# Gathered experts in a two-stream diffusion trunk: the weighted sum of the second halves moved from VectorE rows to TensorE column quarters

## The chip, the cores and the metric

One core of a Trainium2 chip runs the whole step in one launch. The metric is device time in microseconds (us). Several executions of the kernel before were timed; one more was recorded by the hardware profiler, and every row shown here is from that one.

## The reference, cut to what matters

Two layers serve a context stream (128 tokens) and a latent stream (512 tokens). Each layer has a token mixer (gated linear attention, short convolution, windowed attention, merged through three gated branches) and then a feed-forward step with 16384 tiny experts (PEER). Each token picks 16 experts in each of 8 heads, 128 in all; an expert is one row of `u_tab` and one row of `v_tab`, 1024 float32 each:

```python
def block(args):
    xb, ib, gb = args                      # tokens, expert numbers, gates
    act = gelu(einsum('td,thkd->thk', xb, u_tab[ib]))
    return einsum('thk,thkd->td', gb * act, v_tab[ib])
```

All data are float32, and the tables differ from layer to layer.

## The kernel before

The program is a Python generator under a tile scheduler: instructions are issued in the order of the text as far as their tiles are free, and each engine then runs its own queue in order. Long side jobs are generators of their own. `tick()` (called after each group of matmuls in the main work) moves a side job forward by its rate, a number of steps per tick.

Of the five blocks of 128 tokens (one of the context, four of the latents) two take the *gather* way in each layer: the context block and the first latent block. That makes four gathers. The other three latent blocks take the *dense* way (`peer_dense`, L1032 and on): for every pair of expert rows, TensorE forms the hidden values (`u_hidden`, 24 matmuls into a PSUM tile `pb`), multiplies them with a gate map `G`, splits them in two (`daH`, `daL`) and adds the second halves up in six PSUM accumulators (`down`, 18 matmuls per expert). Hidden values of the first 108 experts (layer 0) or 64 (layer 1) are formed ahead and come back from DRAM (`da<-sdr`) in the last part of that loop.

A gather (`peer_gather`, L880) has 128 tokens on the 128 partitions. For each of the 128 ranks j, `fetch` (L908) issues an indirect DMA on GpSimd's queue that brings row `eidx[:, j]` of a table, one row per token, into a buffer `grow` of 128 x 1024 (512 KB). A row of `u` is used on VectorE by `u_row` (L914): multiply with `h`, add up into column j of `w`; after 16 ranks ScalarE applies the Gelu. A row of `v` is used by `v_row` (L920): `acc = g * w[:, j] + acc`, again one VectorE instruction. The order is 16 rows of `u`, then rows of `u` and `v` of neighbouring heads in turn by sixteens; `fetch` runs `LAG` = 1 step ahead of the use (L1250), so a gather has 257 steps. Buffers: five `grow` (L1329, L1373), or, in the dense loop, the eight `wraw` buffers that the weights of the dense way use too (L1390).

Where the four gathers run:

- context, layer 0: beside the latents' mixer (`mixer_lat`, rates 0.9 in the linear attention, 5.5 in the attention, 2.464 in the branches), first fetch at 595 us, last use at 1480 us;
- first latent block, layer 0: beside the gate maps (`gate_map`, 48 ticks at a rate of 2.0), then beside the dense loop with a rate that makes it end some ten ticks before the loop (L1391), from 2282 to 3315 us;
- context, layer 1: beside the latents' mixer (rates 0.84, 6.0, 2.08), from 3392 to 4361 us;
- first latent block, layer 1: as in layer 0 (48 ticks and 30 more of `routing_pairs`, rate 1.056; then the dense loop), from 4596 to 5820 us.

PSUM has four kinds of tiles with two buffers each: `pa`, `po`, `pb`, `pt`. In the mixer `pt` takes transposes (those of the attention's probabilities above all); in the dense loop `pa`, `po` and `pt` are the accumulators, and only `pb` is free for hidden values.

Matmuls of the latents run on pairs of rounded halves (`mm3`, L192, three matmuls in place of one). Matmuls on plain float32 operands stand in the trace as two instructions (passes) each. One line of the kernel before, L401, multiplies 16 partitions at a time, once from partition 0 and once from partition 32.

Of the kernel before, what the change touches and what calls it, by code (L numbers as in the profile page):

```python
# [9 lines left out]
F32 = mybir.dt.float32  # L10
F32R = mybir.dt.float32r
BF16 = mybir.dt.bfloat16
I32 = mybir.dt.int32
U32 = mybir.dt.uint32
U8 = mybir.dt.uint8
AF = mybir.ActivationFunctionType
# [27 lines left out]
def kernel(ctx: ExitStack, tc: tile.TileContext, A: dict, O: list):  # L44
# [760 lines left out]
    def routing_pairs(t, vals, idxs, rp, qp, out):  # L805

        vf = vals[t].rearrange("p (h q) k -> p h q k", q=2)
        xf = qp.tile([128, 8, 2, 16], F32, name="xf", bufs=1)  # L810
        V.tensor_copy(xf.rearrange("p h q k -> p (h q k)"), idxs[t].rearrange("p h k -> p (h k)"))
        top = qp.tile([128, 8, 16], F32, name="top", bufs=1)
        pos = qp.tile([128, 8, 16], U32, name="pos", bufs=1)
        for h in range(8):
            cand = qp.tile([128, 136], F32, name="cand", bufs=1)
            V.tensor_add(cand[:, :128].rearrange("p (a b) -> p a b", b=16),
                         vf[:, h, 0, :8, None].to_broadcast([128, 8, 16]),
                         vf[:, h, 1, None, :].to_broadcast([128, 8, 16]))
            V.tensor_scalar(cand[:, 128:], vf[:, h, 0, 8:], vf[:, h, 1, 0:1], None, op0=OP.add)
            top16(top[:, h, :], pos[:, h, :], cand)  # L820
            if h % 2:
                yield
        pf = qp.tile([128, 8, 16], F32, name="pf", bufs=1)
        V.tensor_copy(pf, pos)
        ab = qp.tile([128, 2, 8, 16], U32, name="ab", bufs=1)
        V.tensor_scalar(ab[:, 0], pos, 4, None, op0=OP.logical_shift_right)
        V.tensor_scalar(ab[:, 1], pos, 15, None, op0=OP.bitwise_and)
        abf = qp.tile([128, 2, 8, 16], F32, name="abf", bufs=1)
        V.tensor_copy(abf, ab)

        V.tensor_scalar(pf, pf, -128.0, 0.0, op0=OP.add, op1=OP.max)
        V.tensor_add(abf[:, 0], abf[:, 0], pf)
        V.tensor_sub(abf[:, 1], abf[:, 1], pf)
        sel = rp.tile([128, 2, 8, 16], F32, name="sel%d" % t)
        yield
        for q in range(2):
            for h in range(8):
                oh = qp.tile([128, 16, 16], F32, name="oh", bufs=2)
                V.tensor_tensor(oh, abf[:, q, h, :, None].to_broadcast([128, 16, 16]),
                                iota16[:, None, :].to_broadcast([128, 16, 16]), op=OP.is_equal)  # L840
                nc.gpsimd.tensor_mul(oh, oh, xf[:, h, q, None, :].to_broadcast([128, 16, 16]))  # L841
                V.reduce_sum(sel[:, q, h, :], oh, axis=mybir.AxisListType.X)
                if h % 4 == 3:
                    yield
        flat3 = lambda v: v.rearrange("p h k -> p (h k)")
        eidx = None
        if t == 0:
            eidx = rp.tile([128, 8, 16], I32, name="eidx")
            V.scalar_tensor_tensor(eidx, sel[:, 0], 128.0, sel[:, 1], op0=OP.mult, op1=OP.add)
            eidx = flat3(eidx)  # L850
        gate = rp.tile([128, 8, 16], F32, name="gate%d" % t)
        V.tensor_sub(gate, top, top[:, :, 0:1].to_broadcast([128, 8, 16]))
        act(gate, gate, AF.Exp)
        gs = qp.tile([128, 8], F32, name="gs", bufs=1)
        V.reduce_sum(gs, gate, axis=mybir.AxisListType.X)
        V.reciprocal(gs, gs)
        V.tensor_mul(gate, gate, gs[:, :, None].to_broadcast([128, 8, 16]))
        out[t] = (eidx, flat3(gate), flat3(sel[:, 0]), flat3(sel[:, 1]))
        yield
# [20 lines left out]
    def peer_gather(s, l, t, eidx, gate, gp, out=None, after=None):  # L880
        h = gp.tile([128, D], F32, name="gh", bufs=1)
        def row():
            return gcfg["p"].tile([128, D], F32, tag=gcfg["tag"], name="grow", bufs=gcfg["n"])

        def mrow(j):
            t_ = row()
            m = modrow[l][s.idx, j * D:(j + 1) * D]
            nc.sync.dma_start(t_, bass.AP(tensor=m.tensor, offset=m.offset, ap=[[0, 128], [1, D]]))
            return t_

        sc, sh = mrow(4), mrow(3)
        x = s.x[t]
        if not s.ctx:
            x = row()
            nc.sync.dma_start(x, xdr[s.name][:, t, :])
        i = V.scalar_tensor_tensor(h, sc, 1.0, x, op0=OP.add, op1=OP.mult)
        if after:
            behind(i, after)
        V.tensor_add(h, h, sh)
        acc = gp.tile([128, D], F32, name="gacc", bufs=1)  # L900
        junk = gp.tile([128, D], BF16, name="gjunk", bufs=1)
        w = gp.tile([128, 128], F32, name="gw", bufs=1)

        def pin(i):
            if PIN[gcfg["m"]]:
                tc.keep_in_program_order(i)

        def fetch(tab, j):  # L908
            g = row()
            nc.gpsimd.indirect_dma_start(out=g, out_offset=None, in_=A[tab + str(l)],  # L910
                                         in_offset=bass.IndirectOffsetOnAxis(ap=eidx[:, j:j + 1], axis=0))
            return g

        def u_row(j, g):  # L914
            pin(V.scalar_tensor_tensor(junk, g, 1.0, h, op0=OP.mult, op1=OP.mult, accum_out=w[:, j:j + 1]))  # L915
            if j % 16 == 15:
                ws = w[:, j - 15:j + 1]
                act(ws, ws, AF.Gelu)

        def v_row(j, g):  # L920
            if j % 16 == 0:
                ws = w[:, j:j + 16]
                V.tensor_mul(ws, ws, gate[:, j:j + 16])
            if j == 0:
                pin(V.tensor_scalar(acc, g, w[:, j:j + 1], None, op0=OP.mult))
            else:
                pin(V.scalar_tensor_tensor(acc, g, w[:, j:j + 1], acc, op0=OP.mult, op1=OP.add))  # L927


        rows = []  # L930
        for hd in range(9):
            r = range(hd * 16, hd * 16 + 16)
            rows += [(u_row, "peer_u", j) for j in r if hd < 8] + [(v_row, "peer_v", j - 16) for j in r if hd]
        todo = []
        for i in range(len(rows) + LAG):
            if i < len(rows):
                todo.append(fetch(*rows[i][1:]))
            if i >= LAG:
                use, _, j = rows[i - LAG]
                use(j, todo.pop(0))  # L940
            yield
        if s.ctx:
            peer_add(s, t, [acc], mrow(5), acc)
            normalize(s, [t])
        else:
            out.append(acc)
# [300 lines left out]
    PL = (5, 5, 5, 2, 0)  # L1247
    BG = (0.55, 2.0, 2.8, 3.622, 0.8)
    FL = (0, 1, 0, 1)
    LAG = 1  # L1250
    PIN = (1, 0, 1)
    PU = (0, 0, 0, 3)
    OB = ('APDAPADA', 'APDAPADA')
# [72 lines left out]

    for l in range(DEPTH):
        with pool("g_ctx") as gp:
            gcfg.update(p=gp, tag="grow", n=5, m=0)  # L1329
            with w_pool(2, 2, PL[1]):  # L1330
                if l:
                    lat.open_cv()
                    run(lat.finish(l))
                    e = bg_add(peer_gather(C, l, 0, ro_c[0], ro_c[1], gp, after=lat.end), RATE[l][0], PR[2])
                    mixer_lat(l, e, range(4))
                else:
                    first = First(gp)
                    e = bg_add(first.work(), RATE[0][0], PR[2])
                    mixer_lat(l, e, range(CONV[0], 4), first)
            bg_drain(e)  # L1340
# [4 lines left out]
        with pool("e_lat") as ep:  # L1345
# [24 lines left out]
            with pool("g_lat") as gp, pool("u_lat") as up_:  # L1370
                ucfg.update(p=up_, n=2, pool_l=PU[1 + l])
                with pool("gm") as qp:
                    gcfg.update(p=qp, tag="grow", n=5, m=1)  # L1373

                    def pairs(t):
                        if not more:
                            for _ in routing_pairs(t, vals, idxs, ep, qp, ro):
                                tick()
                    eu[1] = RU[l][1]
                    pairs(0)  # L1380
                    e = bg_add(peer_gather(Lt, l, 0, ro[0][0], ro[0][1], gp, gout), RG[l], PR[1])
                    pairs(1)
                    for t in range(1, 4):
                        if t < 3:
                            pairs(t + 1)
                        gate_map(t, ro[t], qp)
                    bg_drain(eu)
                ucfg["pool_l"] = PU[3]
                with pool("dense") as dp, w_pool(8, 3, PL[3 + l]):
                    gcfg.update(p=wcfg["p"], tag="wraw", n=8, m=2)  # L1390
                    e[1] = (256 + LAG - e[3]) / (256 - AHEAD[l] - 10)  # L1391
                    peer_dense(Lt, l, hH, hL, dp, e, gout, gp)

# [110 lines left out]
```

## Time and profile before

| | us |
|---|---|
| median of three runs | 5888.09 |
| lowest and highest | 5874.39, 5888.82 |
| the profiled execution | 5883.62 |
| its span in the trace | 5881.8 |

The span is what the rows divide up; 1.8 us of the execution lie around it. Busy times of an engine are unions of its instructions. The record of a matmul lasts until its result is out, so one 512 columns wide is 0.39 us long while the next begins 0.23 us after it; a sum of such records over a group is more than the time that they take up.

### The profile page before, as it was taken

To read this page: it belongs to the slowest core of one execution; us is meant where nothing else is said; L and a number is where in the kernel's file an instruction comes from. 1 tells how busy PE (TensorE), PEld (TensorE's weight loads), DVE (VectorE), ACT (ScalarE), POOL (GpSimd) and SP (SyncE) were. 2 spreads that over 40 slices of the span, in tenths; PEclk is the share of its full clock that TensorE was granted. 3 is DMA by queue.
4 is the path that set the end of the run, shared out by engine and by line. 5 is a ranking of instruction groups with operands and counts; after the bars stand their busy time and mean duration, and the time that the engine had idled before them with its cause. 6 is when DMAs were issued, how large, how long until landed. Compare 5 with 4: busy or idle time off the path is not lost. (4 is left out here: it accounts for less than half of the span.)

```text
span 5881.8 us, 79377 instructions
## 1 busy us (share of the span) xinstructions
PE 5283.8 (90%) x28598; PEld 4525.8 (77%) x28598; DVE 4323.4 (74%) x7951; ACT 2052.8 (35%) x3446; POOL 2682.9 (46%) x2207
## 2 busy tenths in 40 slices
PE   8998789998899989989998787899998787899998
PEld 5787677776678888888777676777777787899976
DVE  3327878887544577988776878898778898777777
ACT  2112433321222214763333333343223356433332
POOL 1223544577211133876444455356752567544322
PEclk9999899998999999989999889999998889999999
DMA  6673346787555556889898643578852676788896
GB/s 262 232 251 119 113 154 217 283 303 271 193 198 196 199 216 214 322 313 340 308 310 307 229 147 108 172 260 307 281 195 104 216 253 246 284 273 274 280 322 215
DMA packets 456714, 1395.14 MB, mean 237 GB/s; under 512 B 42880, under 2 KB 184832, under 8 KB 413312
## 3 DMA queue, kind: packets, MB, share of 16 engines
q1 hardware_dynamic: 303248, 833.73, 40.0%
q0 software_dynamic: 153072, 556.34, 27.7%
q8 instruction: 225, 3.69, 0.2%
q14 instruction: 169, 1.38, 0.1%
HBM read 1275.29 MB, written 114.62 MB: 236 GB/s over the span
## 5 line engine op out<-in xcount | busy, mean ns | idle before, releaser
L910 POOL DMA_INDIRECT grow<-in_peer_v_dram,eidx x512 | 654.9, 1279 | 638.9 <-DVE gacc L927 280.6
L910 POOL DMA_INDIRECT grow<-in_peer_u_dram,eidx x512 | 670.8, 1310 | 555.0 <-DVE gjunk L915 190.6
L927 DVE SCALAR_TENSOR_TENSOR gacc<-grow,gw,gacc 128x1024 f32<-128x1024 f32 x508 | 687.2, 1353 | 89.2 <-DMA grow<-in_peer_v_dram,eidx 83.6
L915 DVE SCALAR_TENSOR_TENSOR gjunk<-grow,gh 128x1024 bf16<-128x1024 f32 x512 | 678.1, 1324 | 56.0 <-DMA grow<-in_peer_u_dram,eidx 51.4
L172 ACT ACTIVATE wh<-wraw 128x1024 fp32r<-128x1024 f32 (+1 forms) x388 | 515.8, 1344 | 549.0 <-PE pa L197 225.3
L174 DVE TENSOR_TENSOR wl<-wraw,wh 128x1408 fp32r<-128x1408 f32 (+2 forms) x388 | 574.3, 1483 | 173.5 <-ACT wh L172 171.6
L176 POOL TENSOR_TENSOR wl<-wraw,wh 128x640 fp32r<-128x640 f32 (+1 forms) x260 | 373.6, 1439 | 683.0 <-ACT wh L172 608.9
L196 PE MATMUL acc<-wh,daH 128*128 128x512 f32 x1536 | 614.6, 400 | 56.3 <-ACT daH L110 42.3
L198 PE MATMUL acc<-wh,daL 128*128 128x512 f32 x1536 | 614.8, 401 | 14.5 <-DVE daL L111 14.2
L197 PE MATMUL acc<-wl,daH 128*128 128x512 f32 x1536 | 611.2, 398 | 0.5 <-DVE wl L174 0.5
L196 PE MATMUL pa<-hH,wh 128*128 128x512 f32 x1312 | 538.9, 411 | 33.0 <-DVE th L739 11.0
L198 PE MATMUL pa<-hH,wl 128*128 128x512 f32 x1312 | 533.4, 407 | 5.8 <-DVE wl L174 5.6
L197 PE MATMUL pa<-hL,wh 128*128 128x512 f32 x1312 | 531.8, 405 | 0.4 <-DVE hL L111 0.4
L196 PE MATMUL po<-hH,uH 128*128 128x384 f32 x1376 | 490.1, 356 | 38.8 <-ACT uH L1007 17.1
L198 PE MATMUL po<-hH,uL 128*128 128x384 f32 x1376 | 475.8, 346 | 30.1 <-DVE uL L1009 30.1
L1007 ACT ACTIVATE uH<-uraw 128x1024 fp32r<-128x1024 f32 x256 | 270.7, 1058 | 617.7 <-PE po L197 210.7
L197 PE MATMUL po<-hL,uH 128*128 128x384 f32 x1376 | 473.8, 344 | 0.0
L1009 DVE TENSOR_TENSOR uL<-uraw,uH 128x1024 fp32r<-128x1024 f32 (+1 forms) x256 | 291.9, 1140 | 139.3 <-ACT uH L1007 118.1
L196 PEld LDWEIGHTS acc<-wh,daH 128*128 128x128 f32 x1536 | 296.5, 193 | 126.7 <-ACT daH L110 53.1
L198 PEld LDWEIGHTS acc<-wh,daL 128*128 128x128 f32 x1536 | 296.1, 193 | 92.4 <-DVE daL L111 30.6
L197 PEld LDWEIGHTS acc<-wl,daH 128*128 128x128 f32 x1536 | 296.3, 193 | 62.3 <-DVE wl L174 1.0
L1056 DVE TENSOR_TENSOR da<-da,G 128x384 f32<-128x384 f32 x256 | 184.2, 748 | 207.8 <-ACT da L1049 202.4
(364 smaller groups left out, 12347.8 us busy)
## 6 DMA issues: line engine op xcount, KB each, us to landing
wraw<-in_w_in_dram SPq DMA_DIRECT2D x168, 1024.0 KB
uraw<-in_u_T_dram SPq DMA_DIRECT2D x256, 512.0 KB
wraw<-in_v_n_dram SPq DMA_DIRECT2D x256, 512.0 KB
wraw<-in_w_mod_dram SPq DMA_DIRECT2D x48, 1024.0 KB
wraw<-in_w_branch_dram SPq DMA_DIRECT2D x48, 1024.0 KB
gdr<-stage SPq DMA_DIRECT2D x24, 2048.0 KB
G<-gdr SPq DMA_DIRECT2D x64, 768.0 KB
sdr<-ust SPq DMA_DIRECT2D x172, 192.0 KB
```

Source lines behind the costliest of these rows:

```text
L172: act(H, raw, AF.Copy)
L174: V.tensor_sub(L[:, :m], raw[:, :m], H[:, :m].bitcast(F32))
L176: nc.gpsimd.tensor_sub(L[:, m:], raw[:, m:], H[:, m:].bitcast(F32))
L196: nc.tensor.matmul(out, aH, bH, start=start, stop=False)
L197: nc.tensor.matmul(out, aH, bL, start=False, stop=False)
L198: nc.tensor.matmul(out, aL, bH, start=False, stop=stop)
L910: nc.gpsimd.indirect_dma_start(out=g, out_offset=None, in_=A[tab + str(l)], in_offset=bass.IndirectOffsetOnAxis(ap=eidx[:, j:j + 1], axis=0))
L915: pin(V.scalar_tensor_tensor(junk, g, 1.0, h, op0=OP.mult, op1=OP.mult, accum_out=w[:, j:j + 1]))
L927: pin(V.scalar_tensor_tensor(acc, g, w[:, j:j + 1], acc, op0=OP.mult, op1=OP.add))
L1007: act(uH, raw, AF.Copy)
L1009: V.tensor_sub(uL[:, :m, :], raw[:, :m, :], uH[:, :m, :].bitcast(F32))
L1056: V.tensor_mul(af, af, G[0][:, :, 2 * (i % 2) + f, :])
```

## The change

`routing_pairs` also leaves the expert numbers transposed (`eidxT`: ranks on partitions, tokens along the row). In `peer_gather` the two halves no longer alternate: 128 steps for `u` as before, then one transpose of the weights `w` (by now Gelu times gate), then 128 steps for `v`, one per token. A step fetches the 128 rows of `v` of one token, ranks on partitions, and four matmuls in float32, one for each quarter of 256 columns, multiply them with a stationary operand of 128 x 32 that is zero but for the token's column of weights. Quarter c goes to the column group at 32c of the array and to partitions 32c to 32c+31 of a PSUM tile `pg`. After 32 tokens ScalarE copies `pg` to SBUF and four DMAs on SyncE's queue put the quarters where `acc` has them. `LAG` becomes 3. `pg` is a `pt` tile in the mixer and beside the gate maps, and a `pb` tile in the dense loop.

```diff
@@ routing_pairs
         if t == 0:
             eidx = rp.tile([128, 8, 16], I32, name="eidx")
-            V.scalar_tensor_tensor(eidx, sel[:, 0], 128.0, sel[:, 1], op0=OP.mult, op1=OP.add)
-            eidx = flat3(eidx)
+            ef = qp.tile([128, 8, 16], F32, name="pf", bufs=1)
+            V.scalar_tensor_tensor(ef, sel[:, 0], 128.0, sel[:, 1], op0=OP.mult, op1=OP.add)
+            V.tensor_copy(eidx, ef)
+            p = pt([128, 128])
+            nc.tensor.transpose(p, flat3(ef), idf)
+            eT = rp.tile([128, 128], I32, name="eidxT")
+            V.tensor_copy(eT, p)
+            eidx = flat3(eidx), eT
@@ peer_gather
-        def v_row(j, g):
...
-                pin(V.scalar_tensor_tensor(acc, g, w[:, j:j + 1], acc, op0=OP.mult, op1=OP.add))
...
+        todo = [fetch("peer_u", eidx, j) for j in range(LAG)]
+        for j in range(128):
+            todo.append(fetch("peer_u", eidx, j + LAG) if j + LAG < 128 else fetch("peer_v", eT, j + LAG - 128))
+            pin(V.scalar_tensor_tensor(junk, todo.pop(0), 1.0, h, op0=OP.mult, op1=OP.mult, accum_out=w[:, j:j + 1]))
             if j % 16 == 15:
                 ws = w[:, j - 15:j + 1]
                 act(ws, ws, AF.Gelu)
+                V.tensor_mul(ws, ws, gate[:, j - 15:j + 1])
             yield
+        p = gcfg["ps"]([128, 128], name="pw")
+        nc.tensor.transpose(p, w, idf)
+        wT = gp.tile([128, 128], F32, name="gw", bufs=1)
+        act(wT, p, AF.Copy)
+        acc = gp.tile([128, D], F32, name="gacc", bufs=1)
+        diag = gp.tile([128, D], F32, tag="gh", name="gdiag", bufs=1)
+        nc.gpsimd.memset(diag, 0.0)
+        st = gp.tile([128, 2, 256], F32, tag="gjunk", name="gst", bufs=1)
+        for b in range(4):
+            act(diag[:, ::33], wT[:, 32 * b:32 * b + 32], AF.Copy)
+            pg = gcfg["ps"]([128, 256], name="pg")
+            for i in range(32):
+                j = 32 * b + i
+                if j + LAG < 128:
+                    todo.append(fetch("peer_v", eT, j + LAG))
+                g = todo.pop(0)
+                for c in range(4):
+                    nc.tensor.matmul(pg[32 * c:32 * c + 32, :], diag[:, 32 * i:32 * i + 32],
+                                     g[:, 256 * c:256 * c + 256], start=i == 0, stop=i == 31,
+                                     tile_position=(0, 32 * c), skip_group_check=True)
+                yield
+            act(st[:, b % 2], pg, AF.Copy)
+            for c in range(4):
+                nc.sync.dma_start(acc[32 * b:32 * b + 32, 256 * c:256 * c + 256], st[32 * c:32 * c + 32, b % 2])
@@
-    LAG = 1
+    LAG = 3
@@ mixer (context gather), gate maps, dense loop
-            gcfg.update(p=gp, tag="grow", n=5, m=0)
+            gcfg.update(p=gp, tag="grow", n=5, m=0, ps=pt)
-                    gcfg.update(p=qp, tag="grow", n=5, m=1)
+                    gcfg.update(p=qp, tag="grow", n=5, m=1, ps=pt)
-                    gcfg.update(p=wcfg["p"], tag="wraw", n=8, m=2)
+                    gcfg.update(p=wcfg["p"], tag="wraw", n=8, m=2, ps=pb)
```

## Rows read from the trace of the kernel before

**Rows 1.** The page, part 1: busy us, share of the span, instructions.
```profile
PE 5283.8 (90%) x28598; PEld 4525.8 (77%) x28598; DVE 4323.4 (74%) x7951; ACT 2052.8 (35%) x3446; POOL 2682.9 (46%) x2207
```

**Rows 2.** `grow`'s instructions by stretch: length, DVE, POOL busy (x fetches), clock, DMA, GB/s.
```profile
595.00:1060.00 465.00, 124.23 (x160) 123.26 (x101) 0.93 0.51 168
...
3390.00:4060.00 670.00, 204.66 (x250) 197.30 (x160) 0.96 0.55 183
```

**Rows 3.** By stretch: length; busy PE, PEld, DVE, ACT, POOL; clock, DMA share, GB/s.
```profile
1106.00:1485.00 379.00, 330.79 (x1509) 270.94 (x1508) 308.68 (x313) 82.63 (x73) 271.63 (x185) 0.93 0.83 297
...
2690.00:3330.00 640.00, 597.26 (x2549) 489.21 (x2550) 481.21 (x557) 230.20 (x268) 290.81 (x286) 0.95 0.90 311
...
3900.00:4365.00 465.00, 436.81 (x2074) 353.54 (x2073) 387.30 (x447) 139.59 (x186) 305.29 (x217) 0.97 0.81 279
...
5050.00:5600.00 550.00, 536.89 (x2689) 486.17 (x2690) 401.73 (x433) 196.03 (x239) 236.90 (x191) 0.99 0.84 287
5600.00:5830.00 230.00, 218.78 (x928) 176.00 (x927) 168.62 (x200) 89.19 (x103) 60.49 (x43) 0.97 0.91 315
```

**Rows 4.** Waits of TensorE, 1060 to 1485: us in total, times, longest.
```profile
PE pa L196 <- ACT yH L110: 15.2, 4, 6.6
PE pa L196 <- DVE th L739: 7.9, 3, 6.7
```

**Rows 5.** Waits of TensorE, 2690 to 3330, first row.
```profile
PE acc L196 <- ACT daH L110: 34.6, 20, 3.9
```

**Rows 6.** Line L1049 (ScalarE's Gelu on `da`), 2690 to 3330: idle before it.
```profile
  DMA da<-sdr: 312.7, 53
```

**Rows 7.** The page, part 5: groups, busy us, mean ns, idle before, releaser.
```profile
L910 POOL DMA_INDIRECT grow<-in_peer_v_dram,eidx x512 | 654.9, 1279 | 638.9 <-DVE gacc L927 280.6
...
L927 DVE SCALAR_TENSOR_TENSOR gacc<-grow,gw,gacc 128x1024 f32<-128x1024 f32 x508 | 687.2, 1353 | 89.2 <-DMA grow<-in_peer_v_dram,eidx 83.6
L915 DVE SCALAR_TENSOR_TENSOR gjunk<-grow,gh 128x1024 bf16<-128x1024 f32 x512 | 678.1, 1324 | 56.0 <-DMA grow<-in_peer_u_dram,eidx 51.4
L172 ACT ACTIVATE wh<-wraw 128x1024 fp32r<-128x1024 f32 (+1 forms) x388 | 515.8, 1344 | 549.0 <-PE pa L197 225.3
...
L176 POOL TENSOR_TENSOR wl<-wraw,wh 128x640 fp32r<-128x640 f32 (+1 forms) x260 | 373.6, 1439 | 683.0 <-ACT wh L172 608.9
```

**Rows 8.** Timeline of TensorE, 410: start us, us, engine, line, operation, count.
```profile
410.52 4.15 PE L194 MATMUL pa<-wraw,yH 128*128 128x256 f32 x18 [0.51 <-ACT yH L750]
```

**Rows 9.** Timeline of TensorE around one call of L401, from 507.67.
```profile
507.67 0.28 PE L197 MATMUL pa<-wl,hH 128*128 128x256 f32 x1
507.79 0.28 PE L198 MATMUL pa<-wh,hL 128*128 128x256 f32 x1
508.00 1.13 PE L401 MATMUL pb<-gaT,a 16*128 16x512 f32 x4
509.06 0.51 PE L196 MATMUL pa<-hH,wh 128*128 128x512 f32 x1
509.40 0.39 PE L197 MATMUL pa<-hL,wh 128*128 128x512 f32 x1
509.63 0.39 PE L198 MATMUL pa<-hH,wl 128*128 128x512 f32 x1
```

**Rows 10.** DMA issues, 1106 to 1485: count, median us to landing.
```profile
grow<-in_peer_v_dram,eidx POOLq DMA_INDIRECT x80, 6.3
```

**Rows 11.** Groups by line: ScalarE's Gelu out of a `pb` tile.
```profile
L1053 ACT ACTIVATE da<-pb 128x384 f32<-128x384 f32 x84 | 39.8, 475 | 18.0 <-PE pb L198 13.4 <-DMA gdr<-stage 4.6
```

**Rows 12.** Waits of TensorE, 4595 to 5050, first row.
```profile
PE pt L959 <- DVE sel L842: 16.3, 3, 9.1
```

**Rows 13.** Line L927: who waited for it, us and times.
```profile
  POOL grow L910: 327.1, 138
```

**Rows 14.** Timeline, 5200: one DMA issue on SyncE's queue.
```profile
5200.72 0.33 SPq L1005 DMA_DIRECT2D uraw<-in_u_T_dram  x1
```

More of the change, by code (lines that the diff above doesn't have):

```diff
@@ L899, in peer_gather @@
         V.tensor_add(h, h, sh)
-        acc = gp.tile([128, D], F32, name="gacc", bufs=1)
+        eidx, eT = eidx
         junk = gp.tile([128, D], BF16, name="gjunk", bufs=1)
@@ L906, in pin, with fetch @@
                 tc.keep_in_program_order(i)
-        def fetch(tab, j):
+        def fetch(tab, ix, j):
             g = row()
             nc.gpsimd.indirect_dma_start(out=g, out_offset=None, in_=A[tab + str(l)],
-                                         in_offset=bass.IndirectOffsetOnAxis(ap=eidx[:, j:j + 1], axis=0))
+                                         in_offset=bass.IndirectOffsetOnAxis(ap=ix[:, j:j + 1], axis=0))
             return g
-        def u_row(j, g):
-            pin(V.scalar_tensor_tensor(junk, g, 1.0, h, op0=OP.mult, op1=OP.mult, accum_out=w[:, j:j + 1]))
+        todo = [fetch("peer_u", eidx, j) for j in range(LAG)]
+        for j in range(128):
+            todo.append(fetch("peer_u", eidx, j + LAG) if j + LAG < 128 else fetch("peer_v", eT, j + LAG - 128))
+            pin(V.scalar_tensor_tensor(junk, todo.pop(0), 1.0, h, op0=OP.mult, op1=OP.mult, accum_out=w[:, j:j + 1]))
             if j % 16 == 15:
@@ L918, in u_row @@
                 act(ws, ws, AF.Gelu)
-        def v_row(j, g):
[L921 to L926, printed above, removed]
-                pin(V.scalar_tensor_tensor(acc, g, w[:, j:j + 1], acc, op0=OP.mult, op1=OP.add))
[L930 to L940, printed above, removed]
-            yield
+                V.tensor_mul(ws, ws, gate[:, j - 15:j + 1])
+            yield
+        p = gcfg["ps"]([128, 128], name="pw")
[22 more added lines that the diff above has]
+                nc.sync.dma_start(acc[32 * b:32 * b + 32, 256 * c:256 * c + 256], st[32 * c:32 * c + 32, b % 2])
         if s.ctx:
```

## The prediction, made before the result was known

> **What bounds the kernel now.** I read the share of busy time first: TensorE 90% of the span, VectorE 74% [rows 1]. The change takes from the second and gives to the first, so its worth lies in the stages where the second halves will run, not in the average. The order of steps in the text tells where these are. A gather will first spend 128 steps on `u`. Beside the gate maps of layer 0 it gets 48 ticks x 2.0 = 96 steps, in layer 1 (48 + 30) x 1.056 = 82; so no token of `v` falls there, and VectorE has as many rows as before. All 2 x 128 latent tokens land in the dense loops. In the mixers 101 rows were fetched by 1060 us and 160 by 4060 [rows 2]; 128 steps are over at about 1100 and 3900, so the context tokens fall into 1106 to 1485 and 3900 to 4365, the end of the attention and the branches. These stretches and the dense loops are the next view [rows 3]: TensorE is busy for 331 of 379, 437 of 465, 597 of 640, 537 of 550 and 219 of 230 us, VectorE for 81%, 83%, 75%, 73% and 73%. Idle TensorE in all five: 48 + 28 + 43 + 13 + 11 = 143 us. The granted clock there averages 0.93 to 0.99 (a mix of 2.4 and 1.2 GHz); its missing share is worth at most 27 + 14 + 32 + 6 + 7 = 86 us.
>
> Who ends the idle time: in the branches ScalarE's split of `yin` and VectorE's `th` [rows 4]; in the dense loop of layer 0 ScalarE's `daH` [rows 5], at the end of a chain that begins with a DMA for which ScalarE waits 313 us in that stretch [rows 6], with the DMA engines 0.90 busy [rows 3]. So VectorE holds TensorE back a little, and a DMA chain does so beside it.
>
> **What is removed.** 508 rows x 1.353 us plus four first ones: some 690 us of VectorE [rows 7]. It shortens the span only where TensorE waits for VectorE. Of the 143 us idle I take two thirds as coming back, 95 us (rows on VectorE stand between `th`, `da` and the splits; and where a DMA is late, a token can fill the hole), and 25 of the 86 us of clock: 120 us. Bounds: 0, and 143 + 86 = 229.
>
> **What is added on TensorE.** A float32 matmul over 256 columns is two passes. Eighteen such passes in a row took 4.15 us [rows 8]: at most 4.15 / 18 = 0.23 us a pass, and 0.22 with the last record's overhang off. A token has 4 quarters x 2 = 8 passes, 1.76 us if they follow each other. Do the quarters overlap? No row shows column groups. The nearest is L401, two float32 matmuls on two groups of rows: four passes of 512 columns (0.44 us each by the same price, 1.76 in turn) took 1.13 us [rows 9]. Its place in the stream can be priced too. The matmul before it began at 507.79, at a spacing of 0.12, so the next could have begun at 507.91; the second after it began at 509.40, at a spacing of 0.23, so the stream was back at 509.17. That is 1.26 us for two lanes of 0.88, and 0.38 us for going into the tiled form and back [rows 9]. I take columns to behave as these rows do: a token alone among other matmuls costs 2 x 0.22 + 0.38 = 0.82 us, and each further one right behind it 0.44. Ends: 0.44 (long groups) and 1.76 + 0.38 = 2.14 (no overlap).
>
> In the dense loops a tick gives (259 - 96) / 138 = 1.18 and (259 - 82) / 182 = 0.97 tokens, each between groups of the loop: 0.8 us x 256 = 205 us. In the branches it gives 2.464 and 2.08: pairs, (0.38 + 0.88) / 2 = 0.63 us x 256 = 161 us. Sum 366 us, between 512 x 0.44 = 225 and 512 x 2.14 = 1096.
>
> The Trainium skill has a rule that speaks against my overlap (TensorE: Matmul & The Clock Gate, Part 3, The mechanism): matmuls start and end in program order, so a quarter's second pass would hold up the next quarter. By that rule a token would be 5 passes long where I have 2 (the third rival below); L401's second matmul did start ahead of the first one's second pass, since otherwise four passes would not fit in 1.13 us [rows 9], so the trace disagrees for groups of rows.
>
> **New waits.** (1) TensorE's queue runs in order, so a row that lands late now stops all matmuls behind it, the dense loop's too. A fetch takes 6.3 us to land in the branches [rows 10]. At one step ahead VectorE waited 84 + 51 us for 1024 rows [rows 7]; at three steps ahead, for 512, I take 35 us. Ends: 0 and 0.5 us a token, 256 us. (2) `pg` holds one of two `pb` buffers in the dense loops. The second hidden product of a pair must then wait until ScalarE has emptied the first: 0.48 us [rows 11] up to one `wh` more in front, 1.8 us [rows 7, 11]. Layer 0's ten such pairs are mostly over when the tokens begin; in layer 1 the tokens begin after 46 / 0.97 = 47 ticks, 12 pairs of 32, which leaves 20 pairs: 10 to 36 us, taken 20. In the attention `pt` is halved in the same way for a third of 64 units in one layer, 0.5 us each: 10 us. (3) Between the halves TensorE transposes `w` behind a chain of VectorE and ScalarE; the nearest is the transpose of `sel`, 16.3 us in 3 waits [rows 12]: 4 times 0 to 9, taken 10 in all. Sum 75 us, between 0 and about 350.
>
> **What is moved or costs nothing.** GpSimd issues as many fetches at 1.28 us. They now wait until TensorE has freed a buffer, where they waited for VectorE, 327 us in 138 waits [rows 13]; behind them stand the `wl` parts (1.44 us each [rows 7]) for which TensorE waits. With three steps of lead I cost this at nothing; if the cover goes it is part of (1). SyncE gets 64 more issues of 0.33 us [rows 14], each four behind a ScalarE copy of some 0.48 us [rows 11], and the weight loads queue behind them: 16 times 2 us, hidden by weights that are loaded two or more buffers ahead. ScalarE gets 36 short copies (17 us at 35% busy [rows 1, 11]), GpSimd four memsets (under 3 us each by `wl` [rows 7]), VectorE eight small copies. The last four quarters come to `acc` by DMA beside the last four experts, 72 x 0.23 = 16 us of matmuls [rows 9]. Bytes from DRAM are the same.
>
> **Sum.** 366 - 120 + 75 = +321 us on the profiled 5884 (span 5882 and 2 us around it; 4 us under the median of the runs): 6205. Of the tokens' price I expect a few to share one excursion where rows come late and then together, about 15 us less: 6190.
>
> **The rivals.**
>
> Faster: VectorE, not TensorE, paces the stretches of `v`. For: it is 81 and 83% busy in the branches, and TensorE's waits name it [rows 3, 4]. Then all idle and clock loss come back (229 us) and the 51 us for which VectorE waits for `u` rows at one step of lead go as well [rows 7], while tokens run in long groups at 0.44: 225 - 229 - 51 = -55, 5830. It decides from a token under 0.55 us with no new wait. Against: TensorE is busy for 98% of the dense loop of layer 1, which holds a quarter of the tokens, and ticks give one at a time.
>
> No change: the same grouping and recovery and nothing else, 225 - 229 = -4, 5880; against it speaks what speaks against the faster case.
>
> Quarters in part in turn: five passes, 5 x 0.22 + 0.38 = 1.48 us, 758 us; with 140 us recovered and 75 new, +693, 6575. For: passes of one quarter stand next to each other in the text. Against: L401.
>
> Quarters fully in turn: 1096 - 150 + 75 = +1020, 6905. For: no row shows column groups at work. This is also the way in which the change wouldn't do what it says.
>
> Rows late on TensorE: forecast plus 0.45 us a token, +230, 6420. For: a tick in the branches comes after 24 matmuls, 5.5 us at 0.23 [rows 9], and gives 2.464 steps, so three steps are 6.7 us, hardly over the 6.3 of a landing [rows 10], and there are five buffers. Against: VectorE's small waits now [rows 7].
>
> **How the numbers follow.** Forecast (6040 to 6330) 0.45; rows late 0.17; five passes 0.10; fully in turn 0.06; faster 0.14; no change 0.08. A measurement tells about 0.3% from no change, 18 us here. Faster 0.14, same 0.08, slower 0.78. The range leaves out the faster case and the fully serial one, together 0.20: 5870 to 6590. It takes in the bounds of the new waits and, for the tokens, all but that last case.
>
> **What would show it.** Right: records of L927 gone; on a new line 4096 passes, those of the four quarters starting within some 20 ns of each other; a token's excursion near 0.8 us in the dense loops; TensorE busy near 100% there and its busy time up by some 300 us, with the longer time in the four stretches named and none beside the gate maps. Wrong: passes 0.22 us apart (in turn); TensorE's waits for `grow` above 100 us (rows late); the branches shorter than 379 us (VectorE was the bound).

## The result and the profile after

The changed kernel took 6091.9 us (median of 4 runs, 6080.5 to 6094.4), the kernel before 5888.5 beside it: ratio 1.033 [1.030, 1.037], 204 us slower. The forecast was 6190 us, between 5870 and 6590; the time lies in that range, on the side that was forecast, 98 us below the forecast itself.

Part 1 of the page of the kernel after, against [rows 1]:

```profile
PE 5570.1 (91%) x32702; PEld 4581.8 (75%) x32702; DVE 3641.2 (60%) x7447; ACT 2068.1 (34%) x3491; POOL 2651.7 (44%) x2211
```

VectorE lost 682 us of work, TensorE got 286. The groups of part 5 that answer to [rows 7] and [rows 13] (busy us, mean ns | idle before, releasers):

```profile
L916 POOL DMA_INDIRECT grow<-in_peer_v_dram,eidxT x512 | 572.3, 1118 | 742.9 <-PE pg L949 464.4
...
L949 PE MATMUL pg<-grow,gdiag 128*32 128x256 f32 x4096 | 298.8, 388 | 24.3 <-ACT gdiag L941 15.3 <-DMA grow<-in_peer_v_dram,eidxT 9.0
```

The new line L949 holds 4096 passes, and all its waits together are 24.3 us, 9.0 of them for rows. GpSimd's fetches now wait for TensorE (464 us) where they waited for VectorE.

The four stretches in which the tokens run (first fetch of `v` to the last in each gather), with the columns of [rows 3]:

```profile
1133.00:1475.00 342.00, 338.18 (x2223) 245.36 (x2223) 92.56 (x83) 71.43 (x67) 213.44 (x169) 1.00 0.81 285
2786.00:3344.00 558.00, 547.54 (x3034) 394.68 (x3033) 234.65 (x275) 189.24 (x225) 240.42 (x238) 0.99 0.85 298
4036.00:4460.00 424.00, 413.64 (x2534) 294.55 (x2534) 121.79 (x144) 102.76 (x129) 214.72 (x171) 0.99 0.72 247
5336.00:5990.00 654.00, 649.12 (x3681) 503.12 (x3680) 270.77 (x285) 208.39 (x256) 198.57 (x171) 1.00 0.78 257
```

TensorE is idle for 3.8 + 10.5 + 10.4 + 4.9 = 30 us of 1978 where it was idle for 143 of 2264, and the granted clock, 0.93 to 0.99 in [rows 3], is 0.99 to 1.00. VectorE is busy for 27 to 42% of a stretch, where it was for 73 to 83%. So TensorE has no room left there: whatever it got is in view.

A lone token and a pair on TensorE, timeline, in the dense loop of layer 1 (start us, us, count):

```profile
5503.39 0.34 PE L198 MATMUL pb<-hH,uL 128*128 128x384 f32 x1
5503.66 1.07 PE L949 MATMUL pg<-grow,gdiag 128*32 128x256 f32 x16
5504.66 0.50 PE L196 MATMUL acc<-wh,daH 128*128 128x512 f32 x1
5505.00 0.40 PE L197 MATMUL acc<-wl,daH 128*128 128x512 f32 x1
...
5862.62 0.39 PE L197 MATMUL acc<-wl,daH 128*128 128x512 f32 x1
5862.85 0.39 PE L198 MATMUL acc<-wh,daL 128*128 128x512 f32 x1
5863.17 0.64 PE L949 MATMUL pg<-grow,gdiag 128*32 128x256 f32 x8
5863.74 0.50 PE L196 MATMUL acc<-wh,daH 128*128 128x512 f32 x1
5864.07 0.39 PE L197 MATMUL acc<-wl,daH 128*128 128x512 f32 x1
```

Matmuls of 512 columns follow at 0.23 us, those of 384 at 0.17. After the lone token's predecessor the next could begin at 5862.85 + 0.23 = 5863.08; the second one behind it began at 5864.07, so the stream was back at 5863.84: 0.76 us. The pair: 5505.00 - 0.23 - (5503.39 + 0.17) = 1.21 us. Priced in this way, each from the starts of its neighbours, the some 340 excursions of the trace (a token, or several in a row, between other matmuls) have a median of 0.77 us for one token, 1.21 for two, 1.64 for three. Their sums in the four stretches are 78, 104, 87 and 99 us, some 368 us (four tokens of the third stretch, left out of this, would add some 3), in which the 24 us of waits at L949 are contained: 344 us for the tokens themselves.

Where the 206 us between the two profiled spans (5881.8 and 6088.2) lie. The stages are cut at the same events in each trace: the first record of L401 for the latent tokens, which begins the first row, the first of L764 for the latent tokens, the first on tile `oa`, the first and last matmul into `acc`. Lengths in us, for the two kernels and for four of the versions below:

| stage | before | after | v_no_fetch | no_fetch | fetch_only | route_late |
|---|---|---|---|---|---|---|
| mixers, layer 0 (context tokens) | 993 | 1007 | 968 | 958 | 973 | 1008 |
| routing of the latent tokens, layer 0 | 858 | 886 | 852 | 875 | 872 | 863 |
| gate maps, layer 0 | 378 | 376 | 358 | 373 | 369 | 388 |
| dense loop, layer 0 (latent tokens) | 681 | 707 | 627 | 594 | 758 | 716 |
| mixers, layer 1 (context tokens) | 1007 | 1068 | 993 | 991 | 1028 | 1063 |
| routing, layer 1 | 325 | 328 | 326 | 327 | 329 | 324 |
| gate maps, layer 1 | 376 | 375 | 366 | 379 | 378 | 386 |
| dense loop, layer 1 (latent tokens) | 798 | 878 | 786 | 777 | 827 | 878 |

After minus before: 14 + 26 + 61 + 80 = 181 us in the four stages with tokens, 28 us in a stage with none (the routing of layer 0), nothing in the other three; ahead of the first stage the changed kernel is 3 us earlier.

### The profile page after: what moved, and what is told of

Read it like the earlier page. It is cut to its first block, busy times and chain, and to the rows that moved or that the text cites. A ratio compares the mean times of both kernels' runs of the same rounds, so it can differ in the third digit from the quotient of the medians.

```text
span 6088.2 us, 86756 instructions
## 1 busy us (share of the span) xinstructions
PE 5570.1 (91%) x32702; PEld 4581.8 (75%) x32702; DVE 3641.2 (60%) x7447; ACT 2068.1 (34%) x3491; POOL 2651.7 (44%) x2211
## 5 line engine op out<-in xcount | busy, mean ns | idle before, releaser
L916 POOL DMA_INDIRECT grow<-in_peer_v_dram,eidxT x512 | 572.3, 1118 | 742.9 <-PE pg L949 464.4
L174 DVE TENSOR_TENSOR wl<-wraw,wh 128x1408 fp32r<-128x1408 f32 (+2 forms) x388 | 560.4, 1447 | 468.2 <-ACT wh L172 401.2
L176 POOL TENSOR_TENSOR wl<-wraw,wh 128x640 fp32r<-128x640 f32 (+1 forms) x260 | 386.1, 1485 | 781.1 <-ACT wh L172 763.9
L924 DVE SCALAR_TENSOR_TENSOR gjunk<-grow,gh 128x1024 bf16<-128x1024 f32 x512 | 644.7, 1259 | 50.3 <-DMA grow<-in_peer_u_dram,eidx 47.8
L198 PE MATMUL acc<-wh,daL 128*128 128x512 f32 x1536 | 602.2, 392 | 1.9 <-DVE daL L111 1.9
L994 POOL TENSOR_SCALAR ob<-iota,tt,tt 128x128 f32<-128x128 f32 x192 | 320.7, 1675 | 45.4 <-PE po L1002 19.1
```

Of the source, the lines that this page charges most:

```text
L174: V.tensor_sub(L[:, :m], raw[:, :m], H[:, :m].bitcast(F32))
L176: nc.gpsimd.tensor_sub(L[:, m:], raw[:, m:], H[:, m:].bitcast(F32))
L198: nc.tensor.matmul(out, aL, bH, start=False, stop=stop)
L924: pin(V.scalar_tensor_tensor(junk, todo.pop(0), 1.0, h, op0=OP.mult, op1=OP.mult, accum_out=w[:, j:j + 1]))
L994: (nc.gpsimd if w == "P" else V).tensor_scalar(ob[:, k, :], iota128, TT[1][:, j:j + 1], TT[2][:, j:j + 1], op0=OP.is_equal, op1=OP.mult)
```

## The experiments

**What a token costs on TensorE.** Two versions change the price of the tokens alone, a third their grouping. First, each token's matmuls issued a second time:

```diff
-                for c in range(4):
-                    nc.tensor.matmul(... start=i == 0, stop=i == 31, ...)
+                for r in range(2):
+                    for c in range(4):
+                        nc.tensor.matmul(... start=i + r == 0, stop=i + r == 32, ...)
```

> Each token's four matmuls are issued twice into the same accumulators (the sum comes out doubled). Theory: two more passes of four quarters at once, 2 x 0.216 x 512 = 221 us, nearly all of it exposed since TensorE is 96 to 100% busy where tokens run: 6290, 6250 to 6320. Rival (tokens fill idle time of TensorE): under 6170.

Measured: 6317.3 us, ratio 1.0725 [1.0707, 1.0743], 225 us above the change. 512 x 0.44 = 225: a token right behind another costs 0.44 us, and all of it shows. Second, all four quarters on one group of columns:

```diff
-                    nc.tensor.matmul(pg[32 * c:32 * c + 32, :], ..., tile_position=(0, 32 * c), ...)
+                    nc.tensor.matmul(pg[:32, :], ..., tile_position=(0, 0), ...)
```

> All four quarters go to column group 0 and the same 32 partitions (so the quarters are added up into one and the sum is wrong), as many passes as in the changed kernel. Theory: eight passes follow each other instead of two rounds of four: 6 x 0.216 x 512 = 663 us more: 6750, 6650 to 6800. Rival (the column groups hardly overlap and the records only look so): under 6250.

Measured: 6710.3 us, 1.1403 [1.1376, 1.1431], 618 us above the change. Its timeline, one token between dense matmuls:

```profile
5899.81 1.91 PE L949 MATMUL pg<-grow,gdiag 128*32 128x256 f32 x8
5901.65 0.44 PE L196 MATMUL pb<-hH,uH 128*128 128x384 f32 x1
```

Eight passes in turn take 1.84 us to the next start; on four groups of columns sixteen took 1.00 (5503.66 to 5504.66, above). The quarters do overlap. Third, tokens run two at a time: a step of even number fetches and does nothing on TensorE, the next one issues both tokens' matmuls.

```diff
+                if i % 2 == 0:
+                    yield
+                    continue
+                for k, g in ((i - 1, g0), (i, g)):
```

> The changed kernel with a token's matmuls held back until the next token's row has been asked for, so that tokens run two at a time. Theory: an excursion of one token costs 0.77 us and one of two 1.21, so about 180 lone tokens in the dense loops make 90 excursions fewer, 90 x 0.33 = 30 us: 6060, 6040 to 6080. Rival (shorter effective lead makes TensorE wait): above 6092.

Measured: 6062.0 us, 1.0297 [1.0267, 1.0327], 30 us under the change. Some 180 lone tokens stood in the dense loops, about 90 in each; in pairs they save about 90 trips at 0.33 us (2 x 0.77 - 1.21), 30 us.

**Whether rows come late on TensorE.** The change with one step of lead in place of three:

```diff
-    LAG = 3
+    LAG = 1
```

> The changed kernel with a lead of 1 in place of 3. Theory: a row lands 5.6 to 7.5 us after its issue, and TensorE then waits in order for rows: 1 us or more for each of half the tokens, 6350, 6200 to 6600. Rival (the lead doesn't matter, since steps are far enough apart): within 30 us of 6092.

Measured: 6073.7 us, 1.0311 [1.0293, 1.0328], 18 us under the change, about as little as a measurement can tell: the rival held, and the fear of late rows falls.

**What of the gain is lead or order.** Two versions of the kernel before with the change's lead, the second also with the change's order (all of `u`, then all of `v`, both on VectorE):

```diff
-    LAG = 1
+    LAG = 3
@@ halves_dve only
-        for hd in range(9):
-            ...
+        rows += [(u_row, "peer_u", j) for j in range(128)] + [(v_row, "peer_v", j) for j in range(128)]
```

> The kernel before with a lead of 3 in place of 1. Theory: VectorE's 135 us of waits for rows get shorter, but TensorE seldom waited for them: 5870, 5845 to 5895. Rival (a good part of the 190 us that came back is the longer lead, not the lighter VectorE): under 5830.

> The kernel before with a lead of 3 and all rows of u ahead of all rows of v, both on VectorE. Theory: the order of the halves is worth nothing by itself, 5870, 5840 to 5910. Rival (the order gives the gain that came back, or costs a part of the loss): more than 60 us away from before_lag3.

Measured: 5899.6 us, 1.0018 [0.9999, 1.0036], and 5893.9 us, 1.0004 [0.9989, 1.0020]. The first lies 5 us above its range, the second in its range. Neither lead nor order moves the kernel before by more than the measurements scatter.

**The index list's transposition.** The kernel before with the change's new piece of routing (a float copy of the list, its transposition on TensorE, two conversions on VectorE), its result unused:

```diff
+            ef = qp.tile([128, 8, 16], F32, name="pf", bufs=1)
+            V.scalar_tensor_tensor(ef, sel[:, 0], 128.0, sel[:, 1], ...)
+            V.tensor_copy(eidx, ef)
+            p = pt([128, 128])
+            nc.tensor.transpose(p, flat3(ef), idf)
+            V.tensor_copy(eT, p)
```

> The kernel before with the new piece of the routing alone (float expert numbers, their transpose, two copies); the gathers are as before. Theory: the 27 us that the stage between the first mixer and the gate maps lost are a reshuffle that begins with this piece: 5915, 5905 to 5930. Rival (they come from when the first gather ends): 5888, within 8.

Measured: 5921.4 us, 1.0052 [1.0034, 1.0071], 30 us slower; the routing stage of layer 0 takes 889 us, as long as after the change. So I moved the piece of the change into the gather:

```diff
+            if j == 64:
+                V.tensor_copy(ef, eidx)
+            if j == 72:
+                p = gcfg["ps"]([128, 128], name="pe")
+                nc.tensor.transpose(p, ef, idf)
+                V.tensor_copy(eT, p)
```

> The change with the transposition of the index list moved out of the routing stage into the gather (its conversion to float at step 64, its transposition at step 72). Theory (28 us of the loss come from the longer chain in the routing stage): 6064, 6050 to 6080, with the stage from the second latent projection to the gate map within 8 us of the kernel before. Rival (the stage is longer by the rows' buffers or the fetches' lead): 6092, within 10, with that stage still 20 us or more longer.

Measured: 6090.8 us, 1.0340 [1.0319, 1.0360]: the change's own time, although the routing stage is back at 863 us. The table shows where it went: the two gate maps are 12 and 11 us longer than after the change, the dense loop of layer 0 is some 8 us longer. Half of the theory held (the piece lengthens that stage), the other half fell (taking it out there doesn't shorten the kernel). The rows of the routing stage as a whole, before and after:

```profile
1436.20:2294.70 858.50, 796.68 (x4912) 690.57 (x4911) 506.49 (x1783) 194.89 (x400) 180.90 (x201) 0.97 0.58 202
```

```profile
1447.60:2334.00 886.40, 818.83 (x5114) 704.90 (x5113) 484.28 (x1781) 195.68 (x393) 182.38 (x202) 0.97 0.57 198
```

TensorE runs 202 matmuls more in it, 22 us of busy time: the stage took in work that lay in other stages before, it didn't only wait. Why the whole is no shorter when the piece stands elsewhere, these runs don't tell.

**What the rows on VectorE held up.** The change without the tokens' matmuls, VectorE copying eight columns of each row in their place:

```diff
-                for c in range(4):
-                    nc.tensor.matmul(pg[32 * c:32 * c + 32, :], ...)
+                V.tensor_copy(st[:, b % 2, 8 * i:8 * i + 8], g[:, :8])
```

> The changed kernel without the tokens' matmuls: each gathered row of v is touched by one copy of 8 columns on VectorE, and the sum of the second halves is left out. Theory (the tokens' 368 us of TensorE are the loss, and VectorE's relief gives 190 us back): 6092 - 368 = about 5725, 5690 to 5780, so about 160 us under the kernel before. Rival (the loss sits in the order of the halves, in the transposed fetch and in TensorE's waits, not in the matmuls): above 5880.

Measured: 6070.3 us, 1.0306 [1.0282, 1.0329]. A miss by 345 us: with the tokens' work gone the kernel is hardly faster than the change. Waits of VectorE and of TensorE in the dense loop of layer 0, 2703 to 3454 (us in total, times, longest):

```profile
DVE gst L947 <- DMA grow<-in_peer_v_dram,eidxT: 338.3, 83, 9.0
...
PE acc L198 <- DVE daL L111: 58.0, 31, 4.3
PE acc L196 <- ACT daH L110: 41.9, 21, 6.6
```

VectorE now waits in its order for each row to land, and `daL` and the splits behind it come late. The probe had put a new wait on VectorE, so it doesn't measure what it was made for. Two more leave VectorE out of it. One leaves the rows unread, the other doesn't fetch them at all:

```diff
@@ fetch_only and no_fetch
-                for c in range(4):
-                    nc.tensor.matmul(pg[32 * c:32 * c + 32, :], ...)
@@ no_fetch only
-                if j + LAG < 128:
-                    todo.append(fetch("peer_v", eT, j + LAG))
-                g = todo.pop(0)
```

> The change without any work for v: no fetches of v, no matmuls on them, nothing on VectorE in their place; the 128 steps of a gather's second half stay empty, and the sum is left out of the result. Theory (the tokens' matmuls are in full view, about 368 us by their excursions, and the place that VectorE gave up is worth about 190 us): 6092 - 368 = 5724, between 5690 and 5760. Rival (the rows on VectorE held TensorE back little, and part of the tokens fills holes that would be there anyway): 5830 to 5900, with TensorE's idle time in the dense loop of layer 0 near the 43 us it had before.

> As the one before, but with the 512 fetches of v, whose rows nobody reads; the sum is left out. Theory (VectorE's copies made the earlier probe wait, 983 us of waits for rows in its order, not the fetches): 5735, 5700 to 5775, at most 30 us above the kernel without fetches. Rival (the fetches themselves, by GpSimd's 1.1 us each or by DMA time, held the earlier probe at 6070): above 5950.

Measured: 5743.4 us, 0.9751 [0.9732, 0.9770], without the fetches; 5990.6 us, 1.0172 [1.0155, 1.0189], with rows that nobody reads. The first is in its range. The second is a miss, and its rival's time: 247 us for fetches alone, 164 of them in the dense loop of layer 0. That loop of `fetch_only`, 2654 to 3412: first waits of SyncE's queue, of ScalarE, of TensorE:

```profile
SPq L168 <- DMA grow<-in_peer_v_dram,eidxT: 384.9, 58, 12.3
...
ACT da L1058 <- DMA da<-sdr: 389.7, 54, 16.0
...
PE acc L196 <- ACT daH L110: 78.6, 26, 11.4
```

There `grow` shares its buffers with the weights (L168 loads them). SyncE waits until a row has landed before it may load a weight into its place, behind it stand the issues for `da`, and at the end of that chain TensorE waits for `daH`. So this probe, too, moved the waiting for rows to a queue that runs in order; what the fetches cost where a later instruction reads them isn't 247 us.

The last version asks the question the other way round. It is the kernel before with VectorE's 512 row operations left in place and only the fetches gone:

```diff
-                todo.append(fetch(*rows[i][1:]))
+                todo.append(fetch(*rows[i][1:]) if rows[i][1] == "peer_u" else h)
```

> The kernel before, in which the 512 fetches of v are left out and VectorE's row operation reads the resident tile h in their place: VectorE does as much as before, DMA and GpSimd do less; the sum over the rows of v is thus not that of the experts. Theory (of the 146 us between the kernel before and the one without any work for v, VectorE's operations hold most): 5850 to 5890, and TensorE's wait for daH stays above 30 us. Rival (the fetches hold most of it, through the transfers and the queues beside them): 5710 to 5790, and that wait is below 10 us. Between them both have a share.

Measured: 5743.2 us, 0.9750 [0.9725, 0.9775]: the time of `no_fetch`, with VectorE as busy as before. My theory fell. Its page, part 1, and its dense loop of layer 0 beside those of before and of `no_fetch` (columns as in [rows 3]):

```profile
PE 5235.7 (91%) x28598; PEld 4494.8 (78%) x28598; DVE 4315.6 (75%) x7951; ACT 2052.3 (36%) x3446; POOL 2083.4 (36%) x1695
...
2620.00:3247.00 627.00, 610.41 (x2720) 505.15 (x2718) 513.41 (x612) 241.18 (x283) 202.50 (x213) 0.99 0.74 252
```

```profile
2673.00:3354.00 681.00, 636.05 (x2720) 520.89 (x2720) 516.36 (x612) 243.45 (x284) 310.85 (x305) 0.95 0.88 305
```

```profile
2650.00:3244.00 594.00, 593.64 (x2697) 501.55 (x2696) 346.17 (x440) 248.13 (x287) 210.99 (x173) 0.99 0.70 231
```

VectorE's busy time is 513 us with and 516 without the gain; what fell is the share of the DMA engines, 0.88 to 0.74, and with it TensorE's idle time, 45 to 17 us, and the missing clock. Its wait for `daH`, 37.2 us in this loop of the kernel before, is 9.1:

```profile
PE acc L196 <- ACT daH L110: 9.1, 7, 3.7
```

The 33 us between the two loops aren't VectorE's alone: in `v_no_fetch` part of the `u` rows still lies in the dense loop, in `no_fetch` more of them lies beside the gate maps, which are 15 us longer there. `no_fetch` also carries the routing piece, which alone cost 30 us. With this allowed for, VectorE's 690 us of row operations, with no fetches beside them, held the kernel up by between nothing and some 30 us, the fetches by about 145. "The fetches" are here all that goes with them: the transfers, GpSimd's 600 us of issuing them (2682.9 us busy before, 2083.4 in `v_no_fetch`), their hold on buffers that the weights use too, and VectorE's waits for `v` rows, 84 us in [rows 7].

For the dense loop of layer 0 the traces say which of these it is. The transfers that bring `da` back from DRAM form a chain: a new one is issued when VectorE has made `daL` of the last. One round in the kernel before, from its timeline (SyncE, ScalarE, VectorE, SyncE):

```profile
3003.09 0.33 SPq L1048 DMA_DIRECT2D da<-sdr  x1
...
3010.01 0.85 ACT L1049 ACTIVATE da<-da 128x768 f32<-128x768 f32 x1 [6.94 <-DMA da<-sdr]
...
3011.84 0.95 DVE L111 TENSOR_TENSOR daL<-da,daH 128x768 fp32r<-128x768 f32 x1
...
3012.81 0.33 SPq L1048 DMA_DIRECT2D da<-sdr  x1
```

All 53 further issues start like this one, within 0.05 us of the end of a `daL`. From an issue to the Gelu that waits for it the mean of the 54 rounds is 6.4 us, from there to the next issue 3.3; in `v_no_fetch` it is 5.2 and 3.5. So 54 x 1.1, some 60 us, came off the transfers, the loop is 54 us shorter, and the part of a round in which VectorE works is no shorter without the fetches, nor without its rows as well (3.7 in `no_fetch`). In this loop TensorE waited for transfers that the fetches slowed, not for VectorE.

## Why the prediction was right, and where it was off

**The tokens' price: right.** 366 us, less 15 for tokens that share an excursion, were forecast, 344 stand in the records; a lone token 0.77 for 0.82, a pair 1.21 for 1.26, a further one 0.44 for 0.44 (the doubled version: 225 us for 512). What [rows 9] showed of groups of rows holds for groups of columns. The five-pass rival and the serial one fall: the trace's excursions are 0.77, not 1.48, and the serial version costs 618 us more. In the records a token's eight passes start in two rounds of four, 6 to 7 ns apart within a round and some 0.22 us from round to round. The Trainium skill (TensorE: Matmul & The Clock Gate, Part 3, The mechanism) states that matmuls start and end in program order, and the five passes were worked out from this. The trace doesn't contradict the rule: the records don't name the quarters, but if each round takes them in the order of the text, the four matmuls as wholes start and end in order. What fails is the step from the rule to five passes, that a quarter's second pass holds up the next quarter; and L401's passes, which the prediction set against the rule, contradict only that step too.

**Where the tokens lie: right.** All in the dense loops and in the ends of the mixers, TensorE busy for 98 to 99% there, the longer time in those four stages, none at the gate maps. In the dense loops the working can be checked against the version without any work for `v`: 707 - 594 = 113 us for excursions of 104 (their waits among them), 878 - 777 = 101 for 99. In the mixers 49 + 77 = 126 us show of 78 + 87; the other 39 us went into time that TensorE loses there without the tokens as well.

**New waits: too high.** 75 us forecast, 24.3 seen at L949: 9.0 for rows, where 35 was taken, and 15.3 for `gdiag`. The handover between the halves, where 10 was taken, made no wait: neither the transposes of `w` nor the first token of any gather has one. The 15.3 us stand at 2949, 3093 and 5852 us, inside the second halves, where ScalarE sets up the stationary operand for the next 32 tokens; that wait wasn't in the sum. The 30 us for halved PSUM have no row of their own among the waits. The rival of late rows falls with this, and with the version at one step of lead, which is no slower: the margin that I computed between three steps and a landing [rows 10] wasn't what decides. GpSimd waits 464 us for TensorE to free a buffer, so a fetch goes out when a buffer is free, at whatever step it is written.

**What comes back: the step that failed.** I took 120 us, 95 of idle time and 25 of clock. By the stages 368 - 181 = 187 us came back. Of what, the four stages tell, taken whole as in the table and so longer than the stretches of [rows 3] (columns as there), before and after:

```profile
443.00:1436.00 993.00, 872.61 (x4692) 729.68 (x4691) 798.53 (x1297) 325.72 (x514) 555.28 (x418) 0.94 0.60 207
2673.00:3354.00 681.00, 636.05 (x2720) 520.89 (x2720) 516.36 (x612) 243.45 (x284) 310.85 (x305) 0.95 0.88 305
3354.00:4361.00 1007.00, 877.77 (x4607) 725.69 (x4606) 832.23 (x1129) 343.57 (x523) 599.79 (x452) 0.94 0.63 215
5062.00:5860.00 798.00, 784.81 (x3743) 685.52 (x3743) 594.16 (x676) 291.79 (x349) 299.46 (x232) 0.99 0.83 284
```

```profile
441.00:1447.00 1006.00, 924.39 (x5558) 747.11 (x5559) 648.96 (x1194) 331.28 (x525) 519.35 (x421) 0.96 0.59 204
2710.00:3417.00 707.00, 693.02 (x3721) 517.12 (x3721) 345.40 (x440) 240.90 (x287) 312.17 (x301) 0.99 0.82 290
3417.00:4485.00 1068.00, 957.61 (x5634) 752.11 (x5633) 651.59 (x1002) 352.93 (x538) 570.96 (x453) 0.95 0.60 203
5188.00:6066.00 878.00, 872.59 (x4767) 697.32 (x4768) 441.82 (x510) 292.04 (x357) 269.98 (x230) 1.00 0.77 258
```

TensorE was idle for 308 us in them and is for 211, 24 of these the new waits: some 120 us of idle time came back, 25 more than forecast. Its busy time rose by 276 us where the tokens' price is 344: by this difference 68 us came back in matmuls that run faster. The granted clock, read to two digits, rose by 0.02, 0.04, 0.01 and 0.01, which on the lengths before is 20 + 27 + 10 + 8 = 65 us. So the clock was the larger error, 43 us: for 25 I had no reason but caution, while in [rows 3] it is lowest in the stretch where TensorE has most gaps, and the tokens filled gaps.

**Its reason was half wrong.** I put the idle time down to VectorE's rows between `th`, `da` and the splits [rows 4, 5], with a DMA chain beside it [rows 6]. With VectorE's rows and without the fetches the kernel before takes the time of the version with neither, which carries the 30 us of the routing piece, and in the dense loop of layer 0 the chain of transfers accounts for all of the 54 us. So the faster rival, in which VectorE paces these stretches, was not merely unlucky in its price: VectorE at 73 to 83% [rows 3] wasn't, for more than some 30 us, what TensorE waited for. That the time lay in the range, 720 us wide, doesn't speak for the reason.

The change left the fetches as they were, and what TensorE waited for because of them went all the same. In the dense loop of layer 0 this can be seen: an issue for `da` still takes 6.3 us to its Gelu (6.4 before), ScalarE still waits 275.3 us for that DMA (317 before), but the issues lie 10.2 us apart where they lay 9.7, since TensorE has tokens to do as well; only 33 of 53 issues follow a `daL` within 0.05 us, and TensorE hardly waits:

```profile
ACT da L1063 <- DMA da<-sdr: 275.3, 48, 10.4
...
PE acc L196 <- ACT daH L110: 1.1, 1, 1.1
```

How much of the 187 us this is, is known in part. By the table, taking the fetches away from the kernel before gives 105 us in the four stages (54 in this loop, 12 in the other, 39 in the mixers) and some 35 in stages without tokens; taking all work for `v` away gives 159 in the four; the other 28 are tokens that went into time which TensorE loses without them as well. By what way the fetches hold up the mixers and the gate maps, and what VectorE's rows cost while fetches run beside them, no run shows.

**Costed at nothing and wrong: the routing piece.** The list's transposition adds about 30 us to the kernel before, and the stage that holds it is 28 us longer after the change. I had not priced it. Whether it costs this in the change is open: moved to another place, it gave nothing back.

The sum with what was measured: tokens 344 + waits 24 - 187 + 28 in the routing stage - 3 elsewhere = 206, the difference of the spans. Against the forecast's 351 + 75 - 120 = 306: 7 us less for the tokens, 51 less for waits, 67 more come back, 25 for what I hadn't priced. Three terms came out in the change's favour, one against it: 100 us.

None of the versions in which the tokens are summed on TensorE beats the kernel before. The best, in pairs, is 174 us slower. The tokens alone cost 225 us at their lowest price, and that is more than what the fetches held up before (145 us) and than what came back here (187 us).

## What to carry to other kernels

An engine that is 73 to 83% busy beside a full TensorE isn't thereby what TensorE waits for: follow the wait to the end of its chain (here to a DMA behind ScalarE), and, before moving the engine's work, run it on resident data without its transfers. Work that is put onto a TensorE that is over 95% busy shows in full, less the idle time and the missing clock that are there now: here 187 us of these came back, more than the 120 that had been counted on, since the added work fills the gaps. A probe that takes the reader of a transfer away or gives it to another engine moves the waiting for the transfer to the next queue that runs in order, and can then be slower than what it was to relieve.

## What the runs showed of the hardware that was not expected

- Four float32 matmuls of 256 columns on four groups of 32 columns cost what one costs, two passes of 0.22 us: 0.44 us a token in a row, 1.21 us less (618 / 512) than on one group.
- Going into that form and back costs about 0.33 us beside the passes (0.77 - 0.44), whatever the number of tokens: 0.77, 1.21, 1.64.
- 512 gathered fetches that move 268 MB (1395.1 MB with them, 1126.6 without) cost the kernel before 145 us, although the DMA engines were at most 0.91 busy in any of its stretches [rows 3], and TensorE's, VectorE's and ScalarE's busy time fell by 48, 8 and 1 us alone without them (GpSimd's, which issues them, by 600). In the dense loop of layer 0 another stream of transfers took 6.4 us from issue to use with them and 5.2 without.
- The granted clock went with TensorE's idle time, not with what filled it. In the dense loop of layer 0 it is 0.92 of 2.4 GHz with 104 us idle of 758 (`fetch_only`), 0.95 with 45 of 681 (before), and 0.99 with 17 of 627 (`v_no_fetch`, no matmul added) and with 14 of 707 (after, tokens added).
